# Latent attention: high and low parts split at the projections, row maxima respread, masks moved to VectorE in seven heads

## The chip, the cores and the metric

The kernel runs on one core of a Trainium2 chip. The metric is the device time of one launch in microseconds. The kernel before took 2097.57, 2088.43 and 2094.3 us in three runs, median 2094.3. TensorE (PE) multiplies matrices into PSUM; VectorE (DVE), ScalarE (ACT) and GpSimd (POOL) work element by element; SyncE (SP) issues most DMAs.

## The reference, cut to what matters

A decoder trunk of two layers over 1024 positions of width 1024, in float32. Layer 0 mixes tokens by latent attention, layer 1 by a sliding window; both also attend to a memory of 256 rows, and each is followed by a squared-ReLU MLP. The change touches layer 0's latent attention alone:

```
c_q, c_kv, k_r, q_cross = split(hn @ w_in)
q  = (rmsnorm(c_q) @ w_uq).reshape(s, 12, 96)     # 64 without position, 32 rotary
kv = (rmsnorm(c_kv) @ w_ukv).reshape(s, 12, 128)  # 64 key, 64 value
q  = concat(q[:64], rope(q[64:])); k = concat(kv[:64], rope(k_r) for all heads)
p  = softmax(where(causal, q @ k.T * 96 ** -0.5, -1e30))
o  = p @ v
```

## The kernel before, in words

**Exactness by parts.** A float32 product is made of three matmuls in a rounded format (float32r): each operand x is split into a high part (`hi`, a ScalarE copy that rounds) and a low part or rest (`lo`, a VectorE subtraction x - hi), and hi·hi, hi·lo and lo·hi are summed in PSUM. The helper is `split` (lines 96 to 104), `mm3` and `mm3w` multiply.

**Projections.** Features lie on partitions and the 1024 positions on columns. Six matmul groups `pskn` make the keys (two heads of 64 rows to a tile `kn[j]`), eight steps `q_rope`/`q_ropeT` make the rotary query parts (positions on partitions, rotated by VectorE and GpSimd, transposed by TensorE into `qr`), and twelve calls `q_nope(j, i)` make the query parts without position (`qn[j]`, half the positions each). Each result is copied out of PSUM once, in full float32, by ScalarE or VectorE. The weights come in through a tile `wraw` of two buffers: an SP load, a ScalarE copy, a VectorE subtraction (`load_cols`).

**A head's operands.** `head_tiles(h)` (line 870) gathers a head's 96 rows by four DMAs into `q32` and `k32` (one buffer each, in SBUF) and splits them there into `qh, ql, kh, kl`, one of three sets `bufs_[h % 3]`. Row 96 of these holds the constants and, in `qh`, the negated row maxima of the head (`max_row`), so that the score matmuls subtract the maximum themselves. `head_ones` copies the constants' rows for heads 1 and 2 by three DMAs.

**Row maxima.** `row_max(h, i)` multiplies one block of 128 queries with all keys up to it, by the high parts alone, into a PSUM tile `psx` (for i > 3 in the attention loop there is a single one, of two banks), and VectorE reduces it with the causal mask `wide` added (line 915). While `h == 0` (before the loop, where `wide` does not exist yet) it reduces the unmasked columns first (line 912) and adds the mask `dmask` to the last 128. Row i has (i + 1)·128 columns. `max_row(h)` transposes the eight columns of maxima and sends them to row 96 of `qh`.

**The attention loop** runs over `seq`, twelve heads of twelve blocks (h, G, k): 128 keys k against the 512 queries of half G, on or below the diagonal. `scores` makes a block transposed (keys on partitions) by three matmuls; a diagonal block (k >= 4G) has only the queries from k on (512, 384, 256 or 128) and needs a mask on its first 128 columns, either by one more matmul of an identity with the mask (`mask_by_pe`, line 1046) or by a VectorE addition (line 1055). A block of 128 queries waits and is sent with the next one. `probabilities` takes the exponential (ScalarE) into one of 12 tiles `p` and adds the sums up on GpSimd; `values` multiplies the last six blocks' tiles with the values, one block after a batch of six is complete. `sums`, `evac` and four plus two DMAs then bring the row sums and the outputs of a head away; in heads 6 to 11 `rc_mul` multiplies by reciprocal sums, and toward the end `WoHalf` loads and splits the output weights.

**What sets the order.** A scheduler orders each engine's and queue's instructions at compile time, by the program's order and its own estimate of when operands are ready; each then runs its instructions strictly in that order. In the loop `product` and `queued` chain all of TensorE's products and row maxima in the order of the program. The table `WHEN` says where a head's row maxima go: entry (i, d) of head h puts row i (8 is `max_row`) after block d of head h - 1; a negative d lies in head h - 2. Before, row 7 stands at d = -7 (block 5 of head h - 2) and row 6 at -5. `head_tiles(h + 2)` is called at the first block of head h. The buffers of head h + 2 are those of head h - 1. Those of head 2 (pool `hb1`) lie where operands of the projections lay.

Of the kernel before, what the change touches and what calls it, by code (L numbers as in the profile page):

```python
# [14 lines left out]
ALU = mybir.AluOpType  # L15
# [40 lines left out]
def trunk(  # L56
# [813 lines left out]
    def head_tiles(h):  # L870
        r = slice((h % 2) * 64, (h % 2) * 64 + 64)
        q32 = hb.tile([96, S], F32, tag="q32", bufs=1, name=f"q32_{h}")
        k32 = hb.tile([96, S], F32, tag="k32", bufs=1, name=f"k32_{h}")
        nc.sync.dma_start(out=q32[0:64], in_=qn[h // 2][r, :])
        nc.sync.dma_start(out=q32[64:96], in_=qr[h // 4][(h % 4) * 32 : (h % 4) * 32 + 32, :])
        nc.sync.dma_start(out=k32[0:64], in_=kn[h // 2][r, :])
        nc.sync.dma_start(out=k32[64:96], in_=krs)
        qh, ql, kh, kl = bufs_[h % 3]
        if h in (1, 2):
            head_ones(h)  # L880
        split(q32, qh[0:96], ql[0:96])
        split(k32, kh[0:96], kl[0:96])
# [15 lines left out]
    def row_max(h, i):  # L898
# [12 lines left out]
        if h == 0 and i:  # L911
            nc.vector.reduce_max(m, ps[:, : n - P], axis=AX, negate=True)
            least = m
        o, k = (ps[:, n - P : n], dmask) if h == 0 else (ps[:, :n], wide[0][:, S - n :])
# [13 lines left out]
    nc.vector.tensor_copy(krs, krT)  # L928
    for j in range(6):
        if j == 1:  # L930
            wqr = rows(wpair(wu, 3, 384, "wqr", "b"), 3)
            for _ in load_cols(mla_w_uq[0], 3, 96, [(wqr, 64, 32)], g_q):
                pass
        ps = ps2(f"pskn{j}")
        mm3w([ps[:, s] for s in halves],
             [(wkn[kt][0][:, j * P : (j + 1) * P], wkn[kt][1][:, j * P : (j + 1) * P], [(ckh[:, kt, s], ckl[:, kt, s]) for s in halves]) for kt in range(2)])
        nc.vector.tensor_copy(kn[j][:, 0:512], ps[:, 0:512])
        nc.scalar.activation(kn[j][:, 512:1024], ps[:, 512:1024], AF.Copy)
# [4 lines left out]
    def q_nope(j, i):  # L943
        ps = ps1(f"psqn{j}_{i}")
        mm3(ps, [(wqn[kt][0][:, j * P : (j + 1) * P], wqn[kt][1][:, j * P : (j + 1) * P], cTh[:, kt, halves[i]], cTl[:, kt, halves[i]]) for kt in range(3)])
        if i:
            nc.vector.tensor_copy(qn[j][:, halves[i]], ps)
        else:
            nc.scalar.activation(qn[j][:, halves[i]], ps, AF.Copy)
# [10 lines left out]
    def q_ropeT(t):  # L960
# [5 lines left out]
        nc.scalar.activation(kq[1][:, 2:4, sl], pt[:, 0 : 2 * P].rearrange("p (k c) -> p k c", k=2), AF.Copy)  # L966
        nc.scalar.activation(qr[2][:, sl], pt[:, 2 * P : 3 * P], AF.Copy)
# [83 lines left out]
    def probabilities(h, G, k, ps):  # L1051
# [4 lines left out]
        p = at.tile([P, 512], F32, tag="p", bufs=12, name=f"p{h}_{G}_{k}")  # L1056
# [99 lines left out]
    def rc_mul(c):  # L1156
# [32 lines left out]
    for n in range(len(seq) + 2):  # L1189
# [1149 lines left out]
```

## Time and profile before

| | us |
|---|---|
| median of 3 runs (lowest, highest) | 2094.3 (2088.43, 2097.57) |
| the profiled execution | 2092.89 |
| its span, first to last instruction | 2091.1 |
| TensorE busy | 2064.6 |
| VectorE busy | 1431.5 |
| ScalarE busy | 1089.0 |
| GpSimd busy | 267.6 |

Times in the rows are microseconds from the span's start. The key projection begins at 174.7, the rotary steps at 190.7, the query parts at 205.2, the attention loop at 233.3; it ends near 440. A matmul's busy time in a row overlaps the next one's: what it costs the engine is the distance from its start to the next start. The granted clock is 1.00 at 2.4 GHz and 0.50 at 1.2 GHz.

### The profile page before, as it was taken

What the parts mean: (1) busy time and instruction counts of PE and PEld (TensorE: products, weight loads), DVE (VectorE), ACT (ScalarE), POOL (GpSimd) and SP (SyncE); (2) the same over time, 40 slices, a digit from 0 to 9 for tenths busy, and PEclk for the clock granted to TensorE, in tenths of its full rate; (3) what the DMA queues carried; (4) which work ended last, traced back from release to release, by engine and by line L of the source; (5) the groups of instructions that cost most, each with busy time, mean ns of one, the idle gap of its engine ahead of it and who ended that gap; (6) DMA issues with size and microseconds to landing.
All of it is one profiled execution on the core that took longest, in us unless ns stands there. A gap on an engine that the chain in (4) does not pass through costs nothing.

```text
span 2091.1 us, 29609 instructions
## 1 busy us (share of the span) xinstructions
PE 2064.6 (99%) x10067; PEld 1685.6 (81%) x10067; DVE 1431.5 (68%) x2829; ACT 1089.0 (52%) x2359; POOL 267.6 (13%) x363
## 2 busy tenths in 40 slices
PE   9999999999999999999999999999999999999998
PEld 6988777678888888888888878778888888888887
DVE  8766656565977777976557534666977776976565
ACT  7554355466745544444445435776755544444453
POOL 1001276630000000000001133420000000000000
PEclk9999999999999999999999999999999999999999
DMA  6302233342444546944433534542344446944332
GB/s 225 104 1 77 55 73 75 109 153 90 141 151 152 166 151 231 332 132 154 140 116 110 147 101 125 140 137 78 129 151 164 162 146 230 331 139 156 121 117 91
DMA packets 183496, 292.88 MB, mean 140 GB/s; under 512 B 17707, under 2 KB 73456, under 8 KB 183344
## 3 DMA queue, kind: packets, MB, share of 16 engines
q1 hardware_dynamic: 177680, 275.17, 41.8%
q0 software_dynamic: 4144, 13.14, 1.7%
q10 hardware_dynamic: 1520, 2.68, 0.4%
q8 instruction: 79, 1.29, 0.2%
q14 instruction: 73, 0.60, 0.1%
HBM read 187.60 MB, written 81.44 MB: 129 GB/s over the span
## 4 chain that ended last, share of the span: by engine, by line
PE 92%; DVE 3%; issue 2%; DMA 1%; ACT 1%; SPq 0%; POOL 0%; ACTq 0%; DVEq 0%; POOLq 0%
PE psu L1575 6%; PE psu L1573 6%; PE psu L1574 6%; PE psy L1912 6%; PE psy L1911 6%; PE psy L1913 6%; PE psz L1912 4%; PE psz L1911 4%; PE psz L1913 4%; PE psv L1575 4%; PE psv L1573 4%; PE psv L1574 4%; PE pss L1023 3%; PE pswo L111 3%; PE pswo L109 3%; PE pswo L110 3%
## 5 line engine op out<-in xcount | busy, mean ns | idle before, releaser
L1070 POOL TENSOR_TENSOR acc<-p,acc 128x512 f32<-128x512 f32 (+2 forms) x96 | 101.1, 1067 | 50.2 <-ACT p L1057 48.0
L915 DVE CUSTOM_DVE_ANT_0 psx<-psx,wide 128x1024 f32<-128x1024 f32 (+5 forms) x88 | 66.5, 769 | 58.8 <-PE psx L908 57.3
L99 ACT ACTIVATE g<-i 128x512 fp32r<-128x512 f32 x79 | 49.9, 631 | 104.1 <-PE psy L1912 50.9
L1911 PE MATMUL psy<-g 128*128 128x512 f32 x256 | 100.0, 390 | 0.0
L1912 PE MATMUL psy<-g 128*128 128x512 f32 x256 | 99.7, 389 | 0.0
L1913 PE MATMUL psy<-g 128*128 128x512 f32 x256 | 99.6, 389 | 0.0
L1057 ACT ACTIVATE p<-pss 128x512 f32<-128x512 f32 (+3 forms) x144 | 65.6, 487 | 52.4 <-PE pss L1023 36.9
L100 DVE TENSOR_TENSOR g<-i,g 128x512 fp32r<-128x512 f32 x79 | 56.1, 710 | 52.0 <-ACT g L99 52.0
L99 ACT ACTIVATE uh<-i 128x512 fp32r<-128x512 f32 x66 | 41.7, 631 | 85.6 <-PE psz L1912 38.6
L99 ACT ACTIVATE i<-mr 128x512 fp32r<-128x512 f32 x78 | 47.7, 627 | 72.5 <-PE psu L1574 20.9
L100 DVE TENSOR_TENSOR uh<-i,uh 128x512 fp32r<-128x512 f32 x66 | 45.5, 690 | 46.8 <-ACT uh L99 46.7
L1911 PE MATMUL psz<-g 128*128 128x512 f32 x192 | 74.7, 389 | 0.0
L1912 PE MATMUL psz<-g 128*128 128x512 f32 x192 | 74.7, 389 | 0.0
L1913 PE MATMUL psz<-g 128*128 128x512 f32 x192 | 74.7, 389 | 0.0
L1472 ACT ACTIVATE mr<-mr,gcol 128x256 f32<-128x256 f32 (+1 forms) x160 | 64.0, 475 | 10.4 <-DMA mr<-in_mlp_w_up_dram 8.3
L100 DVE TENSOR_TENSOR i<-mr,i 128x512 fp32r<-128x512 f32 x78 | 53.5, 686 | 23.0 <-ACT i L99 23.0
L2031 POOL TENSOR_TENSOR wsr<-wsr,gcol 128x1024 f32<-128x1024 f32 x12 | 24.8, 2067 | 344.0 <-ACT i L99 274.6
L1793 DVE TENSOR_TENSOR mqq<-mqf,mqq 128x512 f32<-128x512 f32 x64 | 43.0, 685 | 21.1 <-DMA mqf<-in_mlp_w_down_dram 21.0
L1023 PE MATMUL pso<-p,v 128*64 128x256 f32 (+1 forms) x480 | 56.7, 381 | 0.0
L1913 PEld LDWEIGHTS psy<-g 128*128 128x128 f32 x256 | 48.1, 188 | 10.0
L1911 PEld LDWEIGHTS psy<-g 128*128 128x128 f32 x256 | 48.0, 188 | 9.9
L1912 PEld LDWEIGHTS psy<-g 128*128 128x128 f32 x256 | 48.1, 188 | 9.8
(670 smaller groups left out, 6812.9 us busy)
## 6 DMA issues: line engine op xcount, KB each, us to landing
i<-hd SPq DMA_DIRECT2D x154, 256.0 KB
hd<-uh SPq DMA_DIRECT2D x76, 256.0 KB
hd<-ul SPq DMA_DIRECT2D x76, 256.0 KB
mr<-in_mlp_w_up_dram SPq DMA_DIRECT2D x36, 512.0 KB
hd<-x SPq DMA_DIRECT2D x72, 256.0 KB
mr<-hd SPq DMA_DIRECT2D x70, 256.0 KB
d<-in_mlp_w_up_dram SPq DMA_DIRECT2D x32, 512.0 KB
mqf<-in_mlp_w_down_dram SPq DMA_DIRECT2D x32, 512.0 KB
```

The source lines that it names most:

```text
L99: a = nc.scalar.activation(hi, src, AF.Copy)
L100: d = nc.vector.tensor_tensor(lo, src, f32(hi), ALU.subtract)
L915: nc.vector.tensor_tensor_reduce(o, o, k, -1.0, least, ALU.add, ALU.min, accum_out=m)
L1023: last_mm[0:1] = [nc.tensor.matmul(*args, skip_group_check=True, **kw).ins]
L1057: masked[0:1] = [nc.scalar.activation(p[:, c0:], ps, AF.Exp, scale=SC).ins]
L1070: nc.gpsimd.tensor_tensor(a[:, c0:], p[:, c0:], (a if q is None else q)[:, c0:], ALU.add)
L1573: nc.tensor.matmul(ps, wh[:, k, :], xh[:, k, :], start=p in (1, 2, 5) and k == 0, stop=False, skip_group_check=True)
L1574: nc.tensor.matmul(ps, wh[:, k, :], xl[:, k, :], start=False, stop=False, skip_group_check=True)
L1575: nc.tensor.matmul(ps, wl[:, k, :], xh[:, k, :], start=False, stop=k == 3, skip_group_check=True)
L1911: nc.tensor.matmul(ps, ah[:, j, :], bh, start=start, stop=False, skip_group_check=True)
L1912: nc.tensor.matmul(ps, ah[:, j, :], bl, start=False, stop=False, skip_group_check=True)
L1913: nc.tensor.matmul(ps, al[:, j, :], bh, start=False, stop=k == NP - 1, skip_group_check=True)
```

## The change

Queries and keys are split where they leave the projections. A new helper `part(hi, src, dst)` copies a PSUM result to its high part (ScalarE), subtracts (VectorE) into one of four tiles `lo`, and writes that to DRAM (`qn_d`, `kn_d`, `qr_d`, `kr_d`). `kn`, `qn`, `qr` and `krs` now hold high parts. `head_tiles` has no splits: eight DMAs put high parts (SBUF) and rests (DRAM) right into `kh`, `qh`, `kl`, `ql`, and it is called for head 1 in the middle of the query projections, for head 2 at the loop's first block. Rows 7, 6 and 5 of head 1 are computed before the loop. `WHEN` spreads the rest anew, two blocks change place, masks are added by VectorE in heads 2 to 8, and `p` has 14 buffers.

```diff
     def head_tiles(h):
-        q32 = hb.tile([96, S], F32, tag="q32", bufs=1, name=f"q32_{h}")
-        k32 = hb.tile([96, S], F32, tag="k32", bufs=1, name=f"k32_{h}")
-        nc.sync.dma_start(out=q32[0:64], in_=qn[h // 2][r, :])
-        nc.sync.dma_start(out=q32[64:96], in_=qr[h // 4][(h % 4) * 32 : (h % 4) * 32 + 32, :])
-        nc.sync.dma_start(out=k32[0:64], in_=kn[h // 2][r, :])
-        nc.sync.dma_start(out=k32[64:96], in_=krs)
...
-        split(q32, qh[0:96], ql[0:96])
-        split(k32, kh[0:96], kl[0:96])
+        for t, n, rope in ((kh, kn[h // 2][r, :], krs), (qh, qn[h // 2][r, :], qr[h // 4][e, :]), (kl, kn_d[r_, :], kr_d), (ql, qn_d[r_, :], qr_d[e_, :])):
+            nc.sync.dma_start(out=f32(t[0:64]), in_=n)
+            nc.sync.dma_start(out=f32(t[64:96]), in_=rope)
...
-        if h == 0 and i:
+        if not wide and i:
...
+    def part(hi, src, dst, tail=()):
+        hi = hi.bitcast(F32R)
+        lo = lt.tile([P, 512], F32, tag="lo", bufs=4, name="lo")
...
+        nc.scalar.activation(hi, src, AF.Copy)
+        nc.vector.tensor_tensor(lo, src, f32(hi), ALU.subtract)
+        nc.sync.dma_start(out=dst, in_=lo)
+    for e in range(2):
+        part(krs[:, e * 512 : e * 512 + 512], krT[:, e * 512 : e * 512 + 512], kr_d[:, e * 512 : e * 512 + 512])
...
-        nc.vector.tensor_copy(kn[j][:, 0:512], ps[:, 0:512])
-        nc.scalar.activation(kn[j][:, 512:1024], ps[:, 512:1024], AF.Copy)
+        for s in halves:
+            part(kn[j][:, s], ps[:, s], kn_d[j * P : (j + 1) * P, s])
...
-        if i:
-            nc.vector.tensor_copy(qn[j][:, halves[i]], ps)
-        else:
-            nc.scalar.activation(qn[j][:, halves[i]], ps, AF.Copy)
+        part(qn[j][:, halves[i]], ps, qn_d[j * P : (j + 1) * P, halves[i]])
...
-        nc.scalar.activation(kq[1][:, 2:4, sl], pt[:, 0 : 2 * P].rearrange("p (k c) -> p k c", k=2), AF.Copy)
-        nc.scalar.activation(qr[2][:, sl], pt[:, 2 * P : 3 * P], AF.Copy)
+        part(kq[1][:, 2:4, sl], pt[:, 0 : 2 * P].rearrange("p (k c) -> p k c", k=2), qr_d[0 : 2 * P, sl].rearrange("(k p) c -> p k c", p=P))
+        part(qr[2][:, sl], pt[:, 2 * P : 3 * P], qr_d[2 * P : 3 * P, sl])
...
+        if n == 4:
+            head_tiles(1)
         if n == 8:
-            done = max_row(0)
-        if n == 9:
-            with tc.issue_after(done[0]):
-                head_tiles(1)
+            max_row(0)
+        if n > 8:
+            row_max(1, 16 - n)
...
-    blocks = [(1, 0), (0, 0), (1, 4), (0, 1), (1, 5), (1, 1), (0, 2), (1, 6), (0, 3), (1, 2), (1, 7), (1, 3)]
+    blocks = [(1, 0), (0, 0), (1, 4), (0, 1), (1, 5), (1, 1), (0, 3), (1, 2), (0, 2), (1, 6), (1, 7), (1, 3)]
...
-        return k >= 4 * G and (k % 4 < 2 or h in (0, 1, 7, 9, 10, 11))
+        return k >= 4 * G and h in (0, 1, 9, 10, 11)
...
-        p = at.tile([P, 512], F32, tag="p", bufs=12, name=f"p{h}_{G}_{k}")
+        p = at.tile([P, 512], F32, tag="p", bufs=14, name=f"p{h}_{G}_{k}")
...
-        1: ((7, 0), (3, 0), (6, 2), (2, 2), (5, 4), (1, 4), (4, 5), (0, 6), (8, 8)),
-        2: ((7, -4), (6, -3), (5, -2), (4, 0), (3, 1), (2, 2), (1, 3), (0, 4), (8, 6)),
-        3: ((7, -7), (6, -5), (5, -4), (4, -2), (3, 0), (2, 1), (1, 2), (0, 3), (8, 5)),
+        1: ((4, 0), (3, 0), (2, 1), (1, 2), (0, 2), (8, 4)),
+        2: ((7, -8), (6, -5), (5, -4), (4, -1), (3, 0), (2, 1), (1, 2), (0, 2), (8, 4)),
...
-            if h and j == 0 and h + 2 < H:
+            if j == 0 and h + 2 < H:
                 head_tiles(h + 2)
-            if n == 5:
-                with tc.issue_after(masked[0]):
-                    head_tiles(2)
```

## Rows read from the trace of the kernel before

**Rows 1.** The page: busy time, share of the span and instructions of each engine.
```profile
PE 2064.6 (99%) x10067; PEld 1685.6 (81%) x10067; DVE 1431.5 (68%) x2829; ACT 1089.0 (52%) x2359; POOL 267.6 (13%) x363
```
**Rows 2.** Windows: length, busy time by engine (instructions), clock, DMA share, GB/s.
```profile
233.30:265.30 32.00, 29.50 (x153) 22.30 (x153) 20.41 (x40) 14.89 (x29) 17.26 (x20) 0.84 0.32 71
265.30:359.92 94.62, 90.13 (x612) 66.47 (x610) 57.71 (x130) 51.96 (x108) 64.43 (x61) 1.00 0.30 68
359.92:411.10 51.18, 46.41 (x286) 33.42 (x283) 32.65 (x62) 24.94 (x50) 30.00 (x26) 0.90 0.42 119
```
**Rows 3.** Waits of PE in these three stretches: us in total, times, longest.
```profile
PE psx L908 <- DVE m L915: 2.5, 5, 1.2
PE psx L908 <- DVE m L915: 3.8, 6, 0.7
PE psx L908 <- DVE m L915: 4.6, 3, 2.2
```
**Rows 4.** Timeline, PE: start, us, what; a block with mask, one without.
```profile
287.47 0.39 PE L1023 MATMUL pss<-qh,kh 97*128 97x512 f32 x1
288.27 0.33 PE L908 MATMUL psx<-ckl,ckh 96*128 96x384 f32 x1
...
292.64 0.40 PE L1023 MATMUL pss<-qh,kh 97*128 97x512 f32 x1
293.33 0.27 PE L889 MATMUL psxt<-ident,m 128*8 128x128 f32 x1
```
**Rows 5.** Groups of DVE from 172 to 441: busy us, mean ns | idle before.
```profile
L1055 DVE TENSOR_TENSOR pss<-pss,dmaskT 128x128 f32<-128x128 f32 x24 | 6.7, 303 | 1.1 <-PE pss L1023 0.6
L100 DVE TENSOR_TENSOR kl<-k,kh 96x1024 fp32r<-96x1024 f32 x8 | 10.3, 1285 | 2.0 <-ACT kh L99 1.9
L100 DVE TENSOR_TENSOR x<-fa,x 128x256 fp32r<-128x256 f32 x2 | 0.8, 418 | 0.0
```
**Rows 6.** Timeline, PE and DVE: a head's first score; row 7, its reduction, row 6.
```profile
286.49 0.45 PE L1023 MATMUL pss<-qh,kh 97*128 97x512 f32 x1
293.36 0.71 PE L908 MATMUL psx<-kh,qh 96*128 96x512 f32 x2
294.11 1.23 DVE L915 CUSTOM_DVE_ANT_0 psx<-psx,wide 128x1024 f32<-128x1024 f32 x1 [1.61 <-PE psx L908]
295.46 0.68 PE L908 MATMUL psx<-kh,qh 96*128 96x512 f32 x2 [0.67 <-DVE m L915]
```
**Rows 7.** Timeline of PE and SP; DMA's GB/s in 40 slices of 243.0 to 248.5.
```profile
233.30 0.40 PE L1023 MATMUL pss<-qh,kh 97*128 97x512 f32 x1
234.84 0.59 SPq L867 DMA_DIRECT2D kl<-kl  x1
243.35 0.50 SPq L874 DMA_DIRECT2D q<-qn  x1
284.00 2.48 SPq L1122 DMA_DIRECT2D den<-sm  x4
GB/s 0 0 0 0 0 0 0 0 0 0 30 387 119 298 149 298 149 149 298 89 298 149 298 149 119 328 119 328 89 357 89 149 328 0 257 458 268 0 0 0
```
**Rows 8.** Windows, columns as in rows 2: a stand of PE and what followed.
```profile
373.00:377.00 4.00, 1.83 (x12) 1.26 (x12) 3.62 (x7) 1.08 (x4) 3.92 (x3) 1.00 0.90 204
377.00:381.20 4.20, 4.20 (x28) 2.33 (x32) 1.14 (x2) 0.16 (x1) 1.60 (x3) 0.60 0.57 159
```
**Rows 9.** Windows: the key projection, the rotary steps.
```profile
174.70:190.70 16.00, 15.96 (x70) 12.68 (x69) 7.11 (x14) 6.66 (x14) 0.00 (x0) 1.00 0.48 142
190.70:205.20 14.50, 14.50 (x91) 14.29 (x90) 12.56 (x37) 6.50 (x18) 8.13 (x14) 1.00 0.35 98
```
**Rows 10.** Waits of SP's queue from 172 to 262.
```profile
SPq L708 <- DVE wqrl L103: 12.3, 5, 8.6
```
**Rows 11.** Timeline, DVE and PE: a split of query weights, its first use.
```profile
203.45 0.47 DVE L103 SCALAR_TENSOR_TENSOR wqn2l<-wr,gcol,wqn2h 128x256 fp32r<-128x256 f32 x1
207.14 0.39 PE L111 MATMUL psqn<-cTh,wqn2l 128*128 128x512 f32 x1
```

More of the change, by code (lines that the diff above doesn't have):

```diff
@@ L870, in head_tiles @@
     def head_tiles(h):
-        r = slice((h % 2) * 64, (h % 2) * 64 + 64)
-        q32 = hb.tile([96, S], F32, tag="q32", bufs=1, name=f"q32_{h}")
-        k32 = hb.tile([96, S], F32, tag="k32", bufs=1, name=f"k32_{h}")
-        nc.sync.dma_start(out=q32[0:64], in_=qn[h // 2][r, :])
-        nc.sync.dma_start(out=q32[64:96], in_=qr[h // 4][(h % 4) * 32 : (h % 4) * 32 + 32, :])
-        nc.sync.dma_start(out=k32[0:64], in_=kn[h // 2][r, :])
-        nc.sync.dma_start(out=k32[64:96], in_=krs)
+        r, e = slice((h % 2) * 64, (h % 2) * 64 + 64), slice((h % 4) * 32, (h % 4) * 32 + 32)
+        r_, e_ = slice(h * 64, h * 64 + 64), slice(h * 32, h * 32 + 32)
         qh, ql, kh, kl = bufs_[h % 3]
@@ L910, in row_max @@
         least = 3.0e38
-        if h == 0 and i:
+        if not wide and i:
             nc.vector.reduce_max(m, ps[:, : n - P], axis=AX, negate=True)
             least = m
-        o, k = (ps[:, n - P : n], dmask) if h == 0 else (ps[:, :n], wide[0][:, S - n :])
+        o, k = (ps[:, n - P : n], dmask) if not wide else (ps[:, :n], wide[0][:, S - n :])
         nc.vector.tensor_tensor_reduce(o, o, k, -1.0, least, ALU.add, ALU.min, accum_out=m)
@@ L927, in trunk @@
     head_ones(0)
-    nc.vector.tensor_copy(krs, krT)
+    lt = pool("lt")
+    qn_d, kn_d = [dram.tile([H * 64, S], F32, name=f"{e}nd") for e in "qk"]
+    qr_d, kr_d = dram.tile([H * 32, S], F32, name="qrd"), dram.tile([32, S], F32, name="krd")
+    def part(hi, src, dst, tail=()):
+        hi = hi.bitcast(F32R)
+        lo = lt.tile([P, 512], F32, tag="lo", bufs=4, name="lo")
+        n = 1
+        for d in src.shape[1:]:
+            n *= d
+        lo = lo[0 : src.shape[0], :n]
+        if len(src.shape) == 3:
+            lo = lo.rearrange("p (k c) -> p k c", k=src.shape[1])
+        nc.scalar.activation(hi, src, AF.Copy)
[3 more added lines that the diff above has]
+        part(krs[:, e * 512 : e * 512 + 512], krT[:, e * 512 : e * 512 + 512], kr_d[:, e * 512 : e * 512 + 512])
     for j in range(6):
@@ L983, in trunk @@
             row_max(0, i)
+        if n == 4:
+            head_tiles(1)
         if n == 8:
-            done = max_row(0)
-        if n == 9:
-            with tc.issue_after(done[0]):
-                head_tiles(1)
+            max_row(0)
+        if n > 8:
+            row_max(1, 16 - n)
+    lt.release()
     wu2.release()
@@ L1182, in trunk @@
     for h in range(1, H):
-        for i, d in WHEN[min(h, 3)]:
+        for i, d in WHEN[min(h, 2)]:
             ahead.setdefault((h - 1) * NB + d, []).append((h, i))
```

## The prediction

> **What bounds the kernel now.** I read the page's busy times first: TensorE is busy 99% of the span, VectorE 68%, ScalarE 52% [rows 1]. So time can be won in two ways only: fewer TensorE instructions, or less time in which TensorE stands still or runs at its lower clock. The other engines' savings count where TensorE waits for them. Next I cut the part that the change touches, latent attention, into three stretches [rows 2]: the first head and a half (32.00 us), the heads up to the eighth (94.62), and the end of the loop (51.18). TensorE idles 2.50, 4.49 and 4.77 us there (length less busy). The mean granted clocks are 0.84, 1.00 and 0.90, which at two levels, 1.2 and 2.4 GHz, loses (1 - clock) times the length, 5.1, 0 and 5.1 us. Together 11.8 us of idling and 10.2 us of clock: 22.0 us is all that waits can give back here. The waits view has one name for nearly all of the idling: the row-maximum matmul (psx, line 908) waits until VectorE has reduced the one before it out of the single psx tile, 2.5, 3.8 and 4.6 us [rows 3].
>
> **Masks.** Heads 2 to 8 lose their mask matmuls: 4 each in 2 to 6 and 8, all 8 in head 7, so 32. A block of 512 queries with a mask runs from 287.47 to 288.27, 0.80 us from its first start to the next instruction's, one without from 292.64 to 293.33, 0.69 [rows 4]. So 0.11 us each, **3.5 us** off TensorE. VectorE gains 32 additions of 0.30 us [rows 5], and the exponential on ScalarE now waits for them, with the later exponentials queued behind it and the value products waiting for those. I cost that at nothing: the products of a batch come a block or more after its last scores, and VectorE loses more than it gains, since the two splits per head (1.28 us for the keys', as much for the queries') leave this loop. With that cover gone the price would be one addition per block, 8 x 0.30 = 2.4 us a head.
>
> **Row maxima respread.** The largest row (1024 keys) now comes after block 4, the next (896) after block 7. Before, two blocks of 256 queries stood between them: start to start took 2.10 us, from 293.36 to 295.46, because the reduction takes 1.23 us [rows 6]. Now a block of 512 (0.69) and a pair of 512 and 128 (about 0.87) stand between, with 0.46 for its own two matmuls of 512 columns (0.23 each, a third of 0.69) 2.02. So the steady wait of 0.67 us falls to 0.1. From row 5 (768 columns) to row 4 stand 0.35 + 0.35 + 0.87 = 1.6 us; three quarters of that reduction and the same hand-over ask 1.8, so at most 0.2 is left there.
>
> What is late next is the load. Row 7 of a head two ahead now comes about 5.7 us into the head: 292.64 less the head's first score at 286.49 is 6.15 [rows 4, 6], less four masks. The buffers come free only at the head's start, since the loads now land in them directly. Four such loads of the same bytes were issued from 243.35; in the DMA row, whose 40 slices cover 243.0 to 248.5, data flows until slice 37, so to 248.1, 4.7 us after the first issue [rows 7]. SP first issues the four writes of the sums (2.48 us), which begin some 2.5 us before the next head and now come nearer to it, so the loads start up to 0.7 us late and land at 5.4 to 5.6. That just suffices; I leave 0.35 us a head for what misses. The six heads of the middle stretch idle 4.49 us, 0.75 each: 6 x 0.40 gives **2.4 us** (bounds: 4.5 if nothing is late, a loss if the loads are, the last rival).
>
> **The start.** Rows 7, 6 and 5 of head 1 move into the projections, where TensorE never stands, with the same matmuls. That removes the five waits behind one psx tile (2.5 us) and the 5.1 us of clock after them. But head 2's row 7 is now asked for after block 4 of head 0, some 4.7 us after the scores begin (blocks of 0.69 to 0.80, five small rows). Its buffers lie where the projection's operands were, so nothing can be loaded before the last projection matmul; SP then issues three one-row copies, of which the last ended 2.1 us after the scores began (233.30) in the trace [rows 7], and then the four loads, 4.7 us: they land at 6.9. TensorE stands 2.2 us with all later products queued behind that matmul. A stand of 2.17 us in the trace was followed by 3.4 us at 1.2 GHz [rows 8], one of 1.2 us by 10.2 us [rows 2, 3]; I take the middle, 3.4 us lost. 7.6 - 5.6 = **2.0 us** (bounds 7.6 and -0.3).
>
> **The end.** The 2.17 us came where a split, a multiplication by the reciprocal sums and the big reduction stood in one VectorE queue; the split goes and row 7 no longer meets the multiplications. The other two waits (0.78, 1.62) came behind splits of the output weights, which stay, and whose loads may move onto the same rows, since their buffers come free with the last head's loads. Of 4.77 + 5.1 us I take half, **4.9 us** (bounds 9.9 and 0).
>
> **The projections pay.** Each evacuation was one copy on one engine. Now it is a copy on ScalarE, a subtraction on VectorE and a write to DRAM on SP. In the key part VectorE and ScalarE have room (two engines, 16 us, under half busy). In the rotary stretch VectorE is 12.56 us busy of 14.50 [rows 9], and each of six to eight steps adds subtractions of 256 and 128 columns, about 0.42 and 0.30 [rows 5]: 6 x 0.6 in sequence = 3.6 us into 1.9 us of room. 1.7 us of lag, of which the four PSUM tiles hide some; I take **1.5 us** (bounds 0, since the products of query halves could fill in, and the next-to-last rival's). The head splits' removal (four of 1.2 us late in this stage) pays for the six added query subtractions.
>
> The DRAM trip of the rests is hidden: a head's scores come a whole head, some 15 us, after its loads. The loads of high parts are four a head, as many as before; the rests add four issues of about 0.5 us a head on SP [rows 7], behind the needed ones. Without that order each would push row 7 by as much.
>
> **Sum.** 3.5 + 2.4 + 2.0 + 4.9 - 1.5 = 11.3 us. The profiled execution took 2092.9 us (span 2091.1 and 1.8 around it): 2081.6, say **2082**. Its time lies 1.4 us under the median shown, which is inside the spread of the three runs, so I add nothing.
>
> **Rivals.** *All waits go* (chance 0.22). The middle stretch already runs at full clock with waits of 0.7 us, so short stands don't cost clock; if head 2's load is in time and the weight splits fall between rows, 22.0 + 3.5 - 1.5 = 24.0 us: 2069. Against it: the three one-row copies.
>
> *The rests choke the rotary stretch* (0.17). Some 40 writes to DRAM share SP's queue with the weight loads, and each waits there for its subtraction. SP already stood 12.3 us in five waits of weight loads for VectorE [rows 10]. The split of the last query weights that the first product needs began at 203.45 and took 0.47; the product used it at 207.14 [rows 11]: 3.2 us of slack. Nine loads, each later by one step's 0.72 us of subtractions, make 6.5: a stand of 3.3, 3.4 of clock after it, and the lag of 1.5, 8.2 in all; 12.8 - 8.2 = 4.6: 2088. The Trainium skill, "DMA: Bandwidth & Descriptors", section "Anatomy of one DMA — SWDGE (gpsimd) path", says that a DMA's semaphore wait is held by the sequencer that issues it, so what stands behind it in the queue waits too. By that rule this rival's order alone decides; the waits of SP in the trace agree that weight loads stand there.
>
> *The loads miss row 7 in every head* (0.14), the one that ends slower. If reciprocal loads, sums' writes or evacuations stand before them on SP, they land at about 7.9 instead of 5.5 us; TensorE then stands 2.2 us, and 1.7 us of clock go with it, in heads 2 to 11: 39 us. 2092.9 - 24.0 + 39 = 2108. It decides from about 1.2 us of lateness, where the trace shows the clock falling; below that it only eats into the gain. For it: SP's issues per head rise from ten to fourteen. Against it: the four measured loads.
>
> **Chances and range.** Forecast 0.47, own range 2075 to 2089. A measurement of this kernel can tell 0.5%, 10.5 us, from no change, so faster means under 2083.8. Of the forecast's 0.47 some 0.29 lie there, with all of the first rival and a little of the second: 0.54. Slower (over 2104.8) holds most of the last rival, 0.12. Same: 0.34. The range for 8 in 10 runs from 2069, all waits gone, to 2097, which leaves out the last rival's bulk and the tails.
>
> **What would show it.** Masks: 40 mask matmuls in place of 72. Rows: idle per middle head 0.3 to 0.4 us, and the waits for psx under 3 us in all. Start: one stand of about 2 us, released by a DMA into head 2's key or query tile, and a fall of the clock behind it. End: the stand of 2.2 us gone. Rotary stretch: VectorE over 95% busy and TensorE idle 1 to 2 us. Wrong would be: TensorE waiting for a DMA in each head, or over 5 us idle before the scores begin.

## The result, and the profile after

The changed kernel took 2103.5 us (median of 7 runs, 2101.42 to 2105.45) beside 2094.3 for the kernel before: ratio 1.0046, 95% interval 1.0032 to 1.0060. Forecast were 2082 us, with a range that ended at 2097. The profiled execution took 2102.95 us. Its page, first row:

```profile
PE 2064.4 (98%) x10035; PEld 1685.8 (80%) x10035; DVE 1426.0 (68%) x2869; ACT 1075.0 (51%) x2349; POOL 254.7 (12%) x363
```

TensorE has 32 instructions fewer, the masks, and is as long busy as before [rows 1]; with a span of 2101.2 us it stands more. Stretches of the loop after: the first head, heads 1 to 7, head 8, heads 9 and 10. A head is counted here from the copy of one head's outputs (`evac`) to the next one's, the first from its first score. Where TensorE waits, the text calls it a stand. (Columns as in [rows 2].)

```profile
240.00:266.13 26.13, 21.66 (x111) 15.88 (x110) 10.78 (x27) 8.29 (x18) 10.85 (x14) 0.80 0.47 123
266.13:369.82 103.69, 100.76 (x687) 74.47 (x688) 58.69 (x164) 48.37 (x113) 66.08 (x70) 1.00 0.52 124
369.82:396.70 26.88, 17.91 (x99) 12.81 (x100) 11.58 (x28) 7.01 (x17) 10.08 (x10) 0.75 0.44 123
396.70:429.70 33.00, 31.25 (x201) 23.36 (x202) 13.46 (x25) 17.19 (x36) 22.70 (x21) 0.90 0.50 136
```

The kernel before, heads 1 to 7 and head 8:

```profile
258.62:369.33 110.71, 105.87 (x717) 78.39 (x718) 68.62 (x152) 59.90 (x125) 75.49 (x70) 1.00 0.32 76
369.33:389.00 19.67, 17.32 (x103) 12.04 (x104) 13.13 (x26) 9.89 (x19) 12.13 (x11) 0.91 0.50 130
```

Heads 1 to 7 took 110.71 us before and 103.69 now: the gain in the middle came, 7.0 us. Head 8 lost it: 26.88 in place of 19.67, 9 us idle and a clock of 0.75. The waits of TensorE in the loop, in place of [rows 3]:

```profile
PE psx L904 <- DMA ckh<-qr: 9.0, 1, 9.0
PE psxt L885 <- DVE m L911: 3.7, 2, 2.0
PE psx L904 <- DMA qh<-qr: 1.6, 2, 1.1
PE psx L904 <- DVE m L911: 1.5, 1, 1.5
PE psx L904 <- DMA qh<-kq: 1.5, 2, 1.0
PE psx L904 <- DMA ckh<-kq: 0.7, 2, 0.5
```

The wait of row maxima for one psx tile is down from 10.8 us in 14 waits to 1.5 in one; a single wait for head 10's operands took 9.0. TensorE's row behind it, and SP's queue ahead of it:

```profile
381.07 1.19 PE L904 MATMUL psx<-ckl,ckh 96*128 96x512 f32 x2 [8.97 <-DMA ckh<-qr]
```

```profile
359.31 4.69 SPq L1159 DMA_DIRECT2D rb<-rcd  x4
364.26 1.30 SPq L1136 DMA_DIRECT2D den<-sm  x2
367.80 1.13 SPq L1159 DMA_DIRECT2D rb<-rcd  x2
368.97 1.26 SPq L1136 DMA_DIRECT2D den<-sm  x2
370.34 3.00 SPq L1159 DMA_DIRECT2D rb<-rcd  x4
373.38 0.69 SPq L877 DMA_DIRECT2D ckl<-kq  x1
375.32 1.08 SPq L1159 DMA_DIRECT2D rb<-rcd  x2
376.45 0.59 SPq L878 DMA_DIRECT2D ckl<-krs  x1
```

Head 10's buffers came free when head 8 began, at 366.1; its first load was issued at 373.38, behind six more loads of reciprocal sums (rb), and its second behind another two. rb has two buffers, so each load waits for a VectorE multiplication: the gaps in the rows (365.56 to 367.80) are those waits. The Trainium skill, "Perfetto Trace Analysis", section "DMA Instruction — HWDGE (DVE, Sync)", says that a DMA's reported start comes after its semaphore wait; these rows agree: the waits are gaps, not busy time. They also agree with the rule that the forecast cites from the Trainium skill, that the issuing sequencer holds the wait; its section is on GpSimd's path, and these loads are SP's.

The other losses. The stretch from the value projection to the first score took 108.1 us (before 102.4; 1.4 of the difference are the row maxima moved there). What follows the loop, to the MLP's first product with `g` (psu<-g; the MLP's products begin some 23 us earlier in every kernel), took 119.9 (117.5). The start lost 0.8: head 0 took 26.13 (25.32), though work had moved out of it. SP's rows there, against [rows 7]:

```profile
239.65 0.55 SPq L867 DMA_DIRECT2D ql<-ql  x1
240.28 2.31 SPq L940 DMA_DIRECT2D qnd<-lo  x3
242.69 0.54 SPq L867 DMA_DIRECT2D kh<-kh  x1
243.28 0.59 SPq L867 DMA_DIRECT2D kl<-kl  x1
244.22 0.50 SPq L877 DMA_DIRECT2D kh<-kq  x1
```

and TensorE's row 7 of head 2:

```profile
249.89 1.22 PE L904 MATMUL psx<-kh,qh 96*128 96x512 f32 x2 [0.95 <-DMA qh<-kq]
```

Three writes of rests, besides the three one-row copies, stood ahead of head 2's loads: the first was issued 4.2 us after the scores began, and row 7 of head 2 started at 249.9, 9.9 us after, where 6.9 was forecast.

**The clock.** Every run lists its span and its mean granted clock; (1 - clock) x span is what the lower level cost (0.001 of clock is 2.1 us; means over all runs). In the six runs of the changed kernel made beside the last experiments that is 19.3 us, for the kernel before, beside it, 9.3. So of the loss of 10.8 us between the means 10.0 is clock, and at full clock the two stand 0.8 us apart.

### The profile page after: what moved, and what is told of

The parts are those of the page before. It is cut to its first block, busy times and chain, and to the rows that moved or that the text cites. A ratio compares the mean times of both kernels' runs of the same rounds, so it can differ in the third digit from the quotient of the medians.

```text
span 2101.2 us, 29756 instructions
## 1 busy us (share of the span) xinstructions
PE 2064.4 (98%) x10035; PEld 1685.8 (80%) x10035; DVE 1426.0 (68%) x2869; ACT 1075.0 (51%) x2349; POOL 254.7 (12%) x363
## 4 chain that ended last, share of the span: by engine, by line
PE 90%; DVE 4%; DMA 3%; ACT 1%; issue 1%; SPq 1%; POOL 0%; DVEq 0%; POOLq 0%; ACTq 0%
PE psy L1923 5%; PE psy L1921 5%; PE psy L1922 5%; PE psu L1583 5%; PE psu L1585 5%; PE psu L1584 5%; PE psz L1923 4%; PE psz L1921 4%; PE psz L1922 4%; PE psv L1583 4%; PE psv L1585 4%; PE psv L1584 4%; PE pss L1037 3%; PE pswo L111 3%; PE pswo L109 3%; PE pswo L110 3%
## 5 line engine op out<-in xcount | busy, mean ns | idle before, releaser
L99 ACT ACTIVATE g<-i 128x512 fp32r<-128x512 f32 x79 | 49.9, 631 | 104.8 <-PE psy L1922 52.5
L1071 ACT ACTIVATE p<-pss 128x512 f32<-128x512 f32 (+2 forms) x144 | 67.1, 489 | 70.6 <-PE pss L1037 43.6
L1084 POOL TENSOR_TENSOR acc<-p,acc 128x512 f32<-128x512 f32 (+2 forms) x96 | 89.6, 938 | 49.4 <-ACT p L1071 46.0
L911 DVE CUSTOM_DVE_ANT_0 psx<-psx,wide 128x640 f32<-128x640 f32 (+3 forms) x85 | 63.1, 757 | 41.1 <-PE psx L904 37.5
L1482 ACT ACTIVATE mr<-mr,gcol 128x256 f32<-128x256 f32 (+1 forms) x160 | 64.0, 476 | 13.7 <-DMA mr<-in_mlp_w_up_dram 13.7
L2041 POOL TENSOR_TENSOR wsr<-wsr,gcol 128x1024 f32<-128x1024 f32 x12 | 23.4, 1949 | 344.7 <-ACT i L99 275.5
L1803 DVE TENSOR_TENSOR mqq<-mqf,mqq 128x512 f32<-128x512 f32 x64 | 43.1, 686 | 19.8 <-DMA mqf<-in_mlp_w_down_dram 19.7
```

What stands on the lines that cost most here:

```text
L99: a = nc.scalar.activation(hi, src, AF.Copy)
L1071: masked[0:1] = [nc.scalar.activation(p[:, c0:], ps, AF.Exp, scale=SC).ins]
L1084: nc.gpsimd.tensor_tensor(a[:, c0:], p[:, c0:], (a if q is None else q)[:, c0:], ALU.add)
L1482: nc.scalar.activation(w[:, k, :], w[:, k, :], AF.Copy, scale=g_mlp[layer][:, k0 + k : k0 + k + 1])
```

## The experiments

Times of stretches, us, from one profile each; the ratio to the kernel before is over 5 to 12 runs. "Before loop" is value projection to first score, "behind" the loop's end to the MLP's first product with `g`.

| kernel | ratio, 95% | before loop | head 0 | 1-7 | 8 | 9 | 10 | 11 | behind |
|---|---|---|---|---|---|---|---|---|---|
| before | 1 | 102.4 | 25.3 | 110.7 | 19.7 | 20.5 | 13.0 | 13.4 | 117.5 |
| after | 1.0046 (1.0032, 1.0060) | 108.1 | 26.1 | 103.7 | 26.9 | 17.0 | 16.0 | 13.6 | 119.9 |
| after, again | 1.0048 (1.0034, 1.0062) | 108.0 | 26.1 | 103.5 | 26.9 | 17.0 | 16.0 | 13.6 | 119.9 |
| e1 | 1.0029 (1.0018, 1.0041) | 108.3 | 25.2 | 103.9 | 15.0 | 29.4 | 11.3 | 13.7 | 117.4 |
| e2 | 1.0051 (1.0039, 1.0064) | 107.5 | 25.6 | 103.6 | 26.6 | 17.1 | 12.8 | 13.6 | 119.9 |
| e4 | 1.0055 (1.0041, 1.0068) | 108.4 | 25.8 | 103.9 | 26.8 | 17.0 | 15.8 | 13.7 | 120.1 |
| e5 | 1.0024 (1.0012, 1.0036) | 107.7 | 23.1 | 103.6 | 28.2 | 17.2 | 14.4 | 13.7 | 118.8 |
| e6 | 1.0012 (1.0002, 1.0022) | 107.8 | 26.5 | 103.8 | 20.7 | 21.9 | 11.3 | 13.3 | 117.6 |
| e7 | 1.0022 (1.0010, 1.0034) | 106.9 | 19.3 | 104.2 | 27.3 | 17.6 | 15.8 | 13.6 | 118.7 |
| e8 | 1.0008 (0.9998, 1.0019) | 107.8 | 26.6 | 105.0 | 25.8 | 16.4 | 12.8 | 13.2 | 117.8 |
| e9 | 0.9992 (0.9978, 1.0005) | 108.2 | 23.1 | 103.8 | 21.8 | 18.7 | 11.3 | 13.7 | 121.4 |
| e10 | 1.0020 (1.0008, 1.0033) | 108.3 | 18.4 | 111.5 | 16.3 | 17.3 | 15.9 | 20.7 | 116.6 |
| e11 | 1.0004 (0.9990, 1.0018) | 103.8 | 21.1 | 103.9 | 28.1 | 17.5 | 16.0 | 13.6 | 120.2 |
| e13 | 0.9996 (0.9980, 1.0012) | 107.7 | 24.7 | 113.1 | 20.9 | 16.5 | 12.8 | 17.6 | 116.8 |
| e14 | 0.9999 (0.9985, 1.0013) | 108.2 | 21.5 | 103.6 | 15.1 | 18.9 | 15.8 | 13.6 | 120.3 |
| e15 | 1.0009 (0.9996, 1.0023) | 107.8 | 24.9 | 103.7 | 15.2 | 23.3 | 14.4 | 13.6 | 118.8 |
| e16 | 0.9993 (0.9976, 1.0010) | 110.3 | 23.3 | 103.8 | 15.1 | 23.4 | 16.0 | 13.6 | 120.4 |
| e17 | 0.9993 (0.9981, 1.0004) | 112.9 | 17.5 | 103.6 | 15.0 | 22.7 | 16.0 | 13.7 | 120.3 |
| e18 | 0.9994 (0.9985, 1.0003) | 112.2 | 17.3 | 103.8 | 15.1 | 22.2 | 16.0 | 13.7 | 120.7 |
| e19 | 0.9955 (0.9940, 0.9969) | 107.0 | 18.4 | 104.8 | 14.6 | 18.1 | 12.8 | 13.3 | 117.5 |

### The stand in head 8: what stands ahead of the loads on SP

**e1**, the multiplications of heads 0 to 5 ten blocks later:

```diff
-            if n == GRP[c + 1] * NB + (9 if c == 2 else 13):
+            if n == GRP[c + 1] * NB + (23, 13, 9)[c]:
```

> The changed kernel with one number changed: the multiplications by the reciprocal sums of heads 0 to 5, and with them the loads of rb, begin ten blocks later, so that all but one or two of these loads stand behind head 10's operand loads in SP's queue. Theory A (head 10's loads were issued late because they stood behind rb loads that waited for VectorE): TensorE's wait of 9.0 us for ckh in head 8 goes (under 1 us is left) and so do the 13.65 us at half clock behind it, which cost 6.8; head 8 takes about 14.5 to 15.5 us instead of 26.88 from evacuation to evacuation. The multiplications now meet VectorE work of heads 8 and 9, which may cost up to 3 us there. Total 9 to 13 us less than the changed kernel: 2091 to 2095. Theory B (the loads into buffers that come free only at a head's start are late by themselves, and the rb loads are beside the point): a wait of 5 to 9 us for head 10's operands stays, total 2100 to 2105.

Head 8 took 15.03 us, and head 9 29.35: the stand went to head 11's operands, 8.0 us. TensorE's row, and SP's ahead of it:

```profile
393.92 1.20 PE L904 MATMUL psx<-kh,qh 96*128 96x512 f32 x2 [8.01 <-DMA qh<-qr]
```

```profile
384.87 1.09 SPq L1159 DMA_DIRECT2D rb<-rcd  x2
386.00 0.59 SPq L877 DMA_DIRECT2D kh<-kq  x1
387.71 1.08 SPq L1159 DMA_DIRECT2D rb<-rcd  x2
388.83 0.59 SPq L878 DMA_DIRECT2D kh<-krs  x1
```

The wait follows the rb loads to whichever head they precede. Theory A holds; its size did not, as the cost moved on.

**e6**, multiplications four blocks apart, each load one step ahead:

```diff
         for n, (j, i) in enumerate(todo):
+            if 0 < n < len(todo) - 1:
+                rbs.append(rc_pair(c, *todo[n + 1]))
...
-            if n + 2 < len(todo):
-                rbs.append(rc_pair(c, *todo[n + 2]))
...
-        if n % 2 or n > 11 * NB:
+        if n % 4 == 2 or n > 11 * NB:
```

> The changed kernel with the six multiplications of heads 0 to 5 four blocks apart (before two), and each load of rb issued one such step ahead of its multiplication, so that no load waits long for VectorE on SP, in head 8 or in head 9. Theory A, as the run before bears it out (ten blocks later, the 9.0 us wait for head 10's operands went, and one of 8.0 us for head 11's came in head 9): both waits are under 1.5 us, heads 8 and 9 take 14.5 to 17 us each, no stand over 2 us is left in them; 10 to 13 us less than the changed kernel, ratio to before 0.998 to 1.000. Rival A2 (any rb load ahead of a head's loads costs the stand, by its transfer and not by its wait): a stand of over 3 us for head 10's or head 11's operands stays, ratio 1.002 to 1.004.

The stands shrank to 2.7 and 1.5 us, and each was still followed by 6.8 us at half clock. Two rb loads (1.13 us) still stood just ahead of head 10's.

**e10**: e9 (below) with the rb loads on GpSimd's queue, `nc.sync` to `nc.gpsimd` in `rc_pair`.

> The kernel with both repairs, and the loads of rb issued from GpSimd's queue instead of SP's. In the kernel with both repairs two rb loads (1.13 us) still stood ahead of head 10's operands on SP, and TensorE waited 2.8 us in head 8 and ran 10.2 us at half clock. Theory A (whatever stands ahead of a head's loads on SP at the head's start is paid in full, since row 7 has no slack): the loads of heads 10 and 11 are issued 1.1 us earlier, as in heads 3 to 9; waits for them are under 1.2 us, heads 8 and 9 take 15 to 16 us each (before 21.83 and 18.74); 8 to 10 us less, ratio to before 0.994 to 0.996. Rival (GpSimd's loads hold up its additions of the probabilities, and the sums or the tiles p come late): TensorE waits for acc or p instead, gain under 4 us, ratio 0.997 to 0.999.

Worse than either theory: head 7 took 22.62 us, the last one 20.7. VectorE's multiplications now wait for the loads, up to 8.2 us, in front of the row reductions; TensorE waited for GpSimd's sums, as the rival had it, only in the last head (4.6 us). VectorE's longest wait, 340 to 440:

```profile
DVE qn L1187 <- DMA rb<-rcd: 17.2, 5, 8.2
```

**e14**: e9 with the steps at `n % 4 == 0` and each rb load issued under `tc.issue_after` the last operand load of the head begun before.

> The kernel with both repairs (loads of rb on SP again), with the steps of the multiplications two blocks later and every rb load held back in the scheduler's order until the last operand load of the head begun before it, so that none stands between a head's start and its loads. Theory A (the order on SP is the whole cause of the stands in heads 8 and 9): waits there under 1.2 us, no half clock in them, 15 to 16 us each in place of 21.83 and 18.74; 8 to 10 us less than the kernel with both repairs, ratio to before 0.994 to 0.997. Rival J (VectorE's multiplications among the row reductions make new waits for m of 1 to 3 us there): gain under 4 us, ratio over 0.997.

Head 8 took 15.07 us at full clock, and SP issues its loads with nothing ahead:

```profile
364.95:380.02 15.07, 14.44 (x99) 10.62 (x99) 11.25 (x25) 6.89 (x16) 10.16 (x10) 1.00 0.60 157
```

```profile
362.05 0.53 SPq L877 DMA_DIRECT2D ckl<-kq  x1
362.62 0.59 SPq L878 DMA_DIRECT2D ckl<-krs  x1
363.31 0.56 SPq L877 DMA_DIRECT2D ckh<-fa  x1
```

So the order on SP is the whole cause of the stand. The time did not follow as expected: 0.9999, like e9. Of the 6.6 us that heads 8 and 9 gained against e9's profile, head 10 gave back 4.5 (15.8 in place of 11.3).

### The start

**e2** places `wide` where it overlaps no tile of rests (`den` and `ones` allocated before it). **e5** issues the copies and the last three writes behind `kh` and `qh`:

```diff
+            if h == 2 and t is qh:
+                head_ones(h)
+                for dst, lo in held:
+                    nc.sync.dma_start(out=dst, in_=lo)
```

> The changed kernel with the mask tile `wide` at other addresses: it no longer overlaps a tile of rests, whose write to DRAM it had to wait for. Theory C (in the start, what TensorE waits for is the loads of head 2; the late reductions of head 1's small rows are only beside that): the waits for m at 242.7 (1.5 us) and 248.6 (2.0 us) go, but row 7 of head 2 is asked for earlier and waits for its load until the same 249.9: one stand of about 4 us, then the same 10 us at half clock, and head 0 ends within 0.7 us of where it did; total 2101 to 2105. Theory D (the late mask is the cause of the start's loss): the waits go, and the half clock with them, 3 to 8 us less: 2095 to 2101.

> The changed kernel with head 2's loads of kh and qh ahead of the three one-row copies and of the last three writes of rests on SP; the tiles of rests are kept through the loop (so `wide` no longer overlaps one), and p has 13 tiles instead of 14. Theory C (the loads bind the start): they are issued about 4 us earlier, from 239.7 to 240.3, and land at about 245; row 7 of head 2, asked for at about 245, waits under 1 us, no stand over 1.2 us is left in the start, and so no 10 us at half clock: 4 to 8 us less than the changed kernel, 2095 to 2100. Rival (the clock falls at the start anyway, since before it fell at the same place with other waits): the waits go but about 10 us at half clock stay; 1 to 3 us less, 2100 to 2103. If 14 tiles for p mattered, every head would be some tenths longer than 14.4 to 15.0 us.

In e2 head 0 took 25.58 us: the loads bind (theory C). The 1.5 us wait at the start stayed, unlike the theory's text, but row 7 of head 2 again started 10.0 us after the scores. In e5 it took 23.05, and no wait for loads is left; the rival's half clock stayed, behind the one stand of 1.53 us. **e15** (e14 with `(4, 2), (3, 2), (2, 3), (1, 4), (0, 4), (8, 6)` for head 1) was to remove that stand:

> The same with the last five row maxima of head 1 two blocks later, so that row 4 is not asked for while VectorE still subtracts rests. The stand of 1.5 us at about 242 goes; if stands of that size bring the half clock, the first head takes 18 to 19 us (it did so in one profile, 18.36, and 23.07 in another with the same stand), so 1.5 to 6.6 us less: ratio lower by 0.0007 to 0.003. Rival: row 4 meets head 2's row 7 on the one psx tile, and the stand only moves: no difference.

It moved: a score now waits 1.8 us for VectorE at the same place, and no gain is seen.

**e9** is e5 and e6 together.

> Both repairs together: the multiplications and their loads spread evenly, and head 2's loads ahead of the one-row copies and the last writes, with the tiles of rests kept. If the two causes are independent, their gains add: the start 3 us (23.05 us in place of 26.13 for the first head), heads 8 and 9 some 10 to 13 us, what lies behind the loop 1 to 2.4: 14 to 17 us less than the changed kernel, ratio to before 0.996 to 0.998, so faster than both kernels. Rival: the gain of one is given back by the other (VectorE later in heads 9 and 10, or the clock): ratio over 0.999.

The gains in the loop add (192.3 us, 203.3 after); the time is 0.9992, level with the kernel before, since the loss ahead of the loop stays, and "behind" grew.

### Ahead of the loop

**e4** subtracts 16 columns of each rest, **e7** leaves out the writes, **e11** both (the heads' rests then come from a tile of zeros in e7 and e11).

```diff
-        nc.vector.tensor_tensor(lo, src, f32(hi), ALU.subtract)
-        nc.sync.dma_start(out=dst, in_=lo)
```

> The changed kernel with each subtraction of a rest done on 16 columns alone (the other columns of the rests are left zero); copies, writes and loads stay. It measures what the subtractions cost VectorE in the projections. Theory E (the 5.7 us by which the stretch from the value projection to the first score grew are 1.2 us of moved row maxima and 4.3 us of VectorE's lag): the stretch shrinks from 108.1 us to about 104 (before 102.4, and 1.2 moved here), and nearly all waits of TensorE for lo, fa and rb in it go. Theory F (the writes to DRAM in SP's queue and the copies on ScalarE, which stay, are what TensorE waits for): it stays at 107 to 108. The heads after it may gain 0 to 4 us more by either theory, since the last writes of rests, and with them head 2's loads, come earlier. Total by E 2095 to 2100, by F 2100 to 2104.

> The changed kernel without the writes of rests to DRAM: the subtractions stay (into two tiles), and the heads' rests are loaded from a tile of zeros in SBUF. The run with short subtractions left the stretch from the value projection to the first score at 108.4 us, with VectorE waiting for the tiles of rests to be written (2.2 and 2.3 us) and the DMA engines 97% busy from 187 to 195; so theory E (VectorE's time) fell. Theory G (VectorE and, through PSUM, TensorE wait until the writes have left the tiles): the stretch shrinks to 104 to 105.5. Theory H (neither; the order in which the scheduler lays the key, rotary and query parts costs it, or the copies on ScalarE): it stays at 107 to 108.5. The start gains besides, as head 2's loads stand behind nothing: the first head as in the run with the loads first, 23 to 24 us.

> The changed kernel without the rests altogether: neither subtractions nor writes; the heads' rests are loaded from a tile of zeros. Alone, shortening the subtractions left the stretch from the value projection to the first score at 108.4 us, and leaving out the writes at 106.9. Theory I (each of the two is hidden by the other: a tile in PSUM is held through copy, subtraction, and the wait for a free tile of rests): the stretch falls to 103.5 to 104.5, which is before's 102.4 with the 1.2 us of moved row maxima. Theory H (neither matters; it is where the scheduler puts the parts, or the moved rows): 106 to 107.

108.4, 106.9 and 103.8 us, against 108.1: alone each part looks nearly free, together they are the whole 4.3. In e4 VectorE waited for its tiles to be written, two of its waits:

```profile
DVE lo L943 <- DMA qnd<-lo: 2.6, 2, 2.2
DVE lo L943 <- DMA qrd<-lo: 2.3, 1, 2.3
```

In the changed kernel VectorE is the full engine there, and TensorE stands 1.24 us in the stretch 195 to 211, in e11 not at all (first row: changed; then e11):

```profile
195.00:211.00 16.00, 14.76 (x84) 13.08 (x83) 15.54 (x49) 6.51 (x19) 8.79 (x15) 1.00 0.67 196
```

```profile
195.00:211.00 16.00, 16.00 (x96) 14.84 (x95) 10.74 (x34) 7.52 (x23) 8.38 (x14) 1.00 0.48 130
```

**e16** (e15 with one tile for both rests of a rotary step), **e17** and **e18** (e14, PSUM freed by one copy):

```diff
-        nc.scalar.activation(hi, src, AF.Copy)
-        nc.vector.tensor_tensor(lo, src, f32(hi), ALU.subtract)
+        nc.scalar.activation(lo, src, AF.Copy)
+        nc.scalar.activation(hi, lo, AF.Copy)
+        nc.gpsimd.tensor_tensor(lo, lo, f32(hi), ALU.subtract)
```

> The same again, with the two rests of each rotary step in one tile instead of two, so that the rotary stretch takes eight tiles of rests fewer. If the wait for a free tile makes a part of the 4.3 us, the stretch from the value projection to the first score falls from 108.2 to 106 to 107.5; by the rival (VectorE's time in the rotary stretch, 7.6 and 8.0 us busy of 8.0 each from 195 to 211, decides once tiles are free), it stays within 0.5 us.

> The kernel with rb behind the head's loads, and each rest made otherwise: ScalarE copies the PSUM result in full into the tile of rests, copies it from there to the high part, and GpSimd subtracts in place, so PSUM is free after one copy of about 0.6 us and VectorE has no rests. Theory I (PSUM held through copy and subtraction is the 4.3 us): the stretch from the value projection to the first score falls from 108.2 to 104 to 105.5, the total by 2 to 4 us. Rival K (GpSimd, with 44 more subtractions of up to 1.3 us beside the rotations, becomes late itself, in the rotary stretch and before the first masks): it stays over 107.5.

> The same, but GpSimd subtracts only the rests of 512 columns (keys and query parts without position), VectorE those of the rotary parts, out of SBUF. Theory I: 104 to 105.5 again, and better than the former if GpSimd was late in the rotary stretch; if VectorE's 7.6 and 8.0 us of 8.0 in that stretch are what is left, 106 to 107.

All three made the stretch longer (110.3, 112.9, 112.2). That PSUM is held too long is thus not shown; which link of copy, subtraction, tile and write costs the 4.3 us stays open.

### The masks

**e8** is the changed kernel, **e13** e10 and **e19** e14, each with the masks of heads 2 to 8 where they were before; **after, again** is the changed kernel once more, run beside e10 and e13.

```diff
-        return k >= 4 * G and h in (0, 1, 9, 10, 11)
+        return k >= 4 * G and (k % 4 < 2 or h in (0, 1, 7, 9, 10, 11))
```

> The changed kernel with the masks of heads 2 to 8 added where they were before (32 of them by matmuls again). If a mask matmul costs the 0.11 us that the blocks of before showed, heads 2 to 6 and 8 take 0.4 to 0.5 us more each and head 7 0.9: 3.5 us in all, ratio to before up by 0.0017. Rival: VectorE's additions delay exponentials and rows by as much, and giving them back to TensorE changes nothing (within 1 us), or gains.

> The kernel with both repairs and rb on GpSimd's queue, with the masks of heads 2 to 8 where they were before. In the changed kernel this cost 1.3 us in heads 1 to 7 and gave back as much in head 8, where TensorE stood anyway. Here no stand hides it: theory M (0.11 us a matmul, 3.5 us in all): ratio up by 0.0010 to 0.0020 against the same kernel with VectorE's masks. Rival (VectorE's additions delay row maxima, so the masks on VectorE gain under 1 us): no difference that can be told.

> The changed kernel once more, beside the experiments, as the measure for their differences: ratio to before 1.003 to 1.006 as it was. If its loss came from the one chip or the one time, under 1.002.

> The kernel with both repairs and every rb load behind the head's operand loads, with the masks of heads 2 to 8 where they were before. Theory M (a mask matmul costs 0.11 us, 3.5 in all, and VectorE's additions nothing): ratio to before up from 0.9999 to 1.001 to 1.002. Theory N (VectorE's additions in front of exponentials and row maxima cost as much as the matmuls or more, and the short waits that they make cost clock): ratio 0.996 to 0.999, with a higher mean granted clock over the runs (0.9942 with VectorE's masks).

Three times the masks on TensorE are the faster: 1.0048 to 1.0008, 1.0020 to 0.9996, 0.9999 to 0.9955. Only the middle pair ran side by side; the others are compared through the kernel before, which ran beside each. Theory M falls; theory N's time holds, and by more than it said, with a mean clock of 0.9972 in place of 0.9942. Its reason, short waits behind VectorE's additions, holds in part only, as the stretches show. e19 took 2082.64 us (2077.44 to 2087.24), faster than both kernels. Heads 1 to 8, first e14, then e19:

```profile
261.39:380.02 118.63, 115.16 (x785) 84.94 (x785) 69.90 (x188) 55.38 (x128) 76.37 (x80) 1.00 0.54 131
```

```profile
256.09:375.50 119.41, 117.95 (x817) 88.70 (x818) 61.15 (x157) 56.34 (x129) 75.97 (x80) 1.00 0.54 130
```

The 32 mask matmuls make TensorE 2.8 us longer busy, but the stretch only 0.8 us longer: without them it idles 3.47 us there, with them 1.46. Its waits in the stretch, in e14:

```profile
PE psx L908 <- DMA qh<-qr: 1.6, 2, 1.1
PE psx L908 <- DMA ckh<-qr: 0.6, 1, 0.6
PE psx L908 <- DMA qh<-kq: 0.6, 1, 0.6
PE psx L908 <- DMA ckh<-kq: 0.6, 2, 0.3
```

and in e19:

```profile
PE psx L908 <- DMA qh<-qr: 1.2, 2, 0.7
PE psx L908 <- DMA qh<-kq: 0.3, 1, 0.3
```

They are all for the loads of row 7: without masks row 7 is asked for sooner, and the loads are no sooner there. ScalarE's exponentials wait longer too, though TensorE shows no wait for them there; their waits for VectorE in the stretch, in e14 and in e19:

```profile
ACT p L1077 <- DVE pss L1075: 21.7, 35, 1.6
```

```profile
ACT p L1077 <- DVE pss L1075: 7.7, 12, 0.8
```

So in the very heads whose masks moved, VectorE's masks still gain 0.8 us. What e19 wins lies outside them: 3.1 us in head 0, 3.0 in head 10, 2.8 behind the loop. Head 0 is not the masks' doing: TensorE stands 1.53 us in both, and 6.8 us at half clock follow in e14, none in e19 (see the last section). In head 10 and behind the loop the stands themselves differ; first e14, then e19:

```profile
401.10 0.37 PE L889 MATMUL psxt<-ident,m 128*8 128x128 f32 x1 [1.83 <-DVE m L915]
431.62 0.77 PE L109 MATMUL pswo<-woq,x 128*128 128x512 f32 x1 [2.01 <-DVE rq L1149]
```

```profile
395.76 0.27 PE L889 MATMUL psxt<-ident,m 128*8 128x128 f32 x1 [0.97 <-DVE m L915]
421.66 0.47 PE L109 MATMUL pswo<-woq,x 128*128 128x512 f32 x1 [0.76 <-DVE rq L1149]
```

Beside e14's two stands lie 6.8 and 3.4 us at half clock, beside e19's none. The other two pairs agree on head 10: 16.0 us and a stand of 1.5 (the changed kernel again) against 12.8 and 1.1 (e8), 15.9 and 2.05 (e10) against 12.8 and 1.22 (e13). At that stand VectorE's queue has a split of output weights ahead of the last two reductions, and it waits for ScalarE's copy, 2.56 us in e14 and 1.28 in e19. Why masks of heads 2 to 8 make it later in head 10 is not shown.

The larger part is the clock. Means over all runs, each less the kernel before that ran beside it:

| | at full clock, us | lost to the clock, us |
|---|---|---|
| changed kernel (6 runs) | +0.8 | +10.0 |
| masks back, e8 (11) | -1.1 | +3.3 |
| SP and start repaired, e14 (12) | -3.6 | +3.7 |
| both, e19 (12) | -6.4 | -3.4 |

Either edit is worth 2 to 5 us at full clock and 6 to 7 us of clock, and they add. A run without a profile gives only its mean clock, so where its falls lay isn't known. In the profiles e14's falls lay at 243, 400 and 431, and e19's has none up to the MLP. Of the 13 profiles with a stand of 1.5 to 2.3 us in head 10, 12 have half clock beside it; of the three with 1.0 to 1.2 us (e8, e13, e19) none.

## Why the prediction was wrong

**Masks** (+3.5 forecast): the step that failed most, 5 to 9 us the wrong way. The price of a matmul was near (0.087 us by the busy times, 0.11 forecast). Wrong was "I cost that at nothing". In the heads whose masks moved, the waits for the loads of row 7, which the text itself had called just sufficient, took back 2.0 of 2.8 us; the 2.4 us a head that it feared did not come. The rest came where it had not looked: a stand for VectorE in head 10 of 1.5 to 2.1 us in place of 1.0 to 1.2, another behind the loop, and the half clock beside them. It had priced the clock at stands from 1.2 us on, but expected no such stand from the masks. What links these stands to the masks is open; that undoing the masks' edit takes the loss away is shown.

**Row maxima respread** (+2.4): right for the waits. TensorE's idle time in heads 1 to 7 fell from 4.84 us to 2.93, and to 1.58 with the masks back. The heads gained more than that, 7.0 us: 1.3 are the masks' part, and 5.7 remain with the masks back, of which 2.5 are less busy time with one matmul fewer. Which part of the change gave these 2.5 is not shown. Heads 1 to 7 of e8:

```profile
265.74:370.73 104.99, 103.41 (x716) 77.72 (x717) 52.71 (x136) 49.23 (x113) 66.53 (x70) 1.00 0.52 124
```

**The end** (+4.9): wrong, heads 8 to 11 took 6.9 us more than before, 3.0 of them in head 10, which went with the masks. The kernel before loaded a head into staging tiles one head ahead; now the loads wait for the head to begin, behind six and then two more loads of rb that wait for VectorE. The third rival had this mechanism, reciprocal loads ahead of the operands on SP, but in every head with 2.2 us; it came in one, with 9.0 us and a stretch of 13.7 us at half clock. The count of SP's issues in that rival had to be made where the multiplications begin, not per head.

**The start** (+2.0, measured -0.8, or -2.2 without the 1.4 us of row maxima that moved out of it): the loads landed 3 us later than forecast, since the last writes of rests weren't counted ahead of them on SP. Putting them first gave 3.1 us back (e5).

**The projections** (-1.5, measured -4.3 without the moved rows): the direction was right (VectorE 15.54 us busy of 16); the size was forecast from VectorE's lag alone. Without subtractions or without writes the stretch stayed within 1.2 us, without both the 4.3 went; which link binds stays open.

**Choked weight loads** (the second rival): not seen; no wait of TensorE for weights, neither before the loop nor in its waits.

**Behind the loop** nothing was forecast; 2.4 us were lost in the changed kernel, where the output projection stands 1.77 us for VectorE (0.53 before). In e1, e6, e8 and e19, where no such stand is over 0.9 us, the stretch took 117.4 to 117.8, about as before.

The parts together are 8.8 of the 10.1 us between the two profiled executions. Another 1.1 lie ahead of the value projection, where the changed kernel's profile has 3.4 us at half clock at 47; 4 of the 20 profiles have that fall, both of the changed kernel among them. It lies ahead of what the change touches, and no run shows why it comes.

## What to carry to other kernels

Before crediting work taken off the busiest engine, ask what it waits for next; if that is a load without slack, the credit turns into short waits. Then ask what the work costs on the engine that gets it, heads later too: here stands of that engine, and the clock beside them, cost more than the work did. When staging buffers are removed, look at every DMA that the queue holds at the moment the real buffers come free, above all those that wait for a computation, and put the operands first. Undo one part at a time and judge it by the whole time over many runs: here the heads whose masks moved show that edit as a gain of 0.8 us, and the loss lay elsewhere.

## What was not expected of the hardware

The same stand does not always bring the lower clock. e9 and e10 have the same program at the start, the same wait of 1.53 us for m and then no other; in e9 10.2 us at half clock follow, in e10 none. The stretches from 1.5 us after it, e9, then e10:

```profile
243.68:256.00 12.32, 12.32 (x54) 9.34 (x52) 3.78 (x10) 3.79 (x9) 6.23 (x6) 0.58 0.43 136
```

```profile
243.02:256.00 12.98, 12.98 (x87) 10.41 (x87) 6.97 (x18) 6.52 (x15) 9.38 (x10) 1.00 0.59 173
```

TensorE started 54 instructions in the one and 87 in the other. So a difference of some 5 us between two profiles of such kernels says little; the means over 5 to 35 runs carried the verdicts here.
